# Strassen's algorithm for all columns of w_down, with accumulating transfers for two of the weight sums

## The chip, the core and the metric

The kernel runs on one core of a Trainium2 chip. The metric is the device time of one execution in microseconds (us). The engines named below are PE (the matrix engine, fed by PEld's weight loads), DVE (elementwise on two inputs), ACT (elementwise on one input, casts), POOL (a general engine) and SP (a queue that issues transfers).

## The reference

An encoder of two layers over 256 tokens of width 2048. The mixers of a layer (projection, three kinds of attention, output projection) are the same before and after the change. What it touches is the MLP that follows them:

```python
h = rmsnorm(x, norm_mlp[l])
u = jax.nn.relu(jnp.einsum('bsd,df->bsf', h, w_up[l]))     # 2048 -> 8192
x = x + jnp.einsum('bsf,fd->bsd', u * u, w_down[l])        # 8192 -> 2048
```

All of it is in float32.

## The kernel before

**Precision.** Every operand of a matmul is split into two parts of a shorter float format (fp32r): hi, a cast on ACT, and lo, the rest, a subtraction on DVE. A product is then three matmuls: hi times hi, lo times hi, hi times lo.

**Steps.** The kernel is one list of steps. A step takes one 512 KB piece of weights (128 partitions x 1024 columns), and does the matmuls with it. The main loop over the steps (from L1016) issues, at step i, the loads of step i + 6 (`load`, SP's queue), the split of the weights of step i + 2 (`split`, L988 the cast into `whi`, L989 the subtraction into `wlo`; each has three buffers), the `prep` of step i + 4 where there is one, and then the matmuls of step i. The framework places the instructions of each engine in a fixed order from this, by their dependences and its own times, so that neighbours can change places; each engine then runs its list in order.

**Groups.** The 8192 hidden columns are worked in eight groups of 1024 per layer. A group's u comes from 16 up steps (four blocks q of 256 columns, four steps each; 8 matmuls of 512 columns, L691, and 8 of 256 columns, L696). After each fourth up step the block is taken out of its two PSUM banks: L668 to L676 form u squared and its two parts, and `sums_of` (L707) forms four sums of u's blocks for Strassen's algorithm. These make up the left operand of w_down in the next round. While group g of w_down is worked, the up steps of group g + 1 run between.

**w_down.** For columns 1024 to 2047 (j = 2, 3) a group has 8 plain steps of 12 matmuls (`mode_b`, L477), which add in two banks per j, then L739 adds them to x. For columns 0 to 1023 of groups 0 to 6 the product of u (2 blocks of 128 tokens by 2 parts of the group's rows) and of the weights (2 parts by 2 column blocks of 512) is done by Strassen's algorithm in Winograd's form, with 7 products instead of 8 (`strassen_steps`). Each product has two steps of 6 matmuls (h = 0, 1, the halves of its rows; L802), and adds up in bank a or d, which share the tile S, or in a bank of its own (P2). After its second step L782 adds it to x, or subtracts it. Products in the order P1, P6, P7, P5, P3, P2, P4; a later product on the same bank goes on adding to what the bank holds. The right operands are weights or sums of them: B12 + B11, B22 + B11 + B12, B12 + B22 and B21 added to the second, all made by DVE (L815, L817, L821, L832) for h = 0 and h = 1.

The raw weights lie in `wraw` (five buffers, up and plain steps), `side` (four buffers: B12, B22, B21) and `spare` (one for each h: B11). `mm_bank` gives one of six banks. `t2` and the parts of u lie in `big` (24 buffers).

**Order of a group before.** 0 is an up or plain step, 1 a step of a product; one round per product:

```python
order = [0, 0]
for p_ in range(7):
    order += [1, 0, 1] + ([0, 0] + [0] * (p_ in (1, 3, 5)) if p_ < 6 else [])
```

Group 7 has plain steps alone, in both versions.

Of the kernel before, what the change touches and what calls it, by code (L numbers as in the profile page):

```python
# [23 lines left out]
P = 128  # L24
# [19 lines left out]
def tile_trunk(ctx: ExitStack, tc: tile.TileContext, x_in, w_in, w_o, w_up, w_down,  # L44
# [459 lines left out]
    def layer_steps(l):  # L504
# [152 lines left out]
        def up_steps(g):  # L657

            out_, evacs = [], []
            for q in range(4 * g, 4 * g + 4):  # L660
                box = {}

                def evac(q=q, box=box):
                    need(("rrow", l))
                    a = mid(F32, 2, 256)
                    for i in range(2):

                        nc.scalar.copy(a[:, i, :], box["b"][i][:, 256:512])  # L668
                        nc.vector.tensor_add(a[:, i, :], a[:, i, :], box["b"][i][:, 0:256])
# [6 lines left out]
                    nc.vector.tensor_sub(u[:, 1], a, f(u[:, 0]))  # L676
                    uT[q] = u
                    if q < 28:
                        sums_of(q, a)
# [27 lines left out]
        def sums_of(q, a):  # L707

            v = a.rearrange("p k (t c) -> p (k t) c", t=2)
            sm = mid(F32, 4, P)  # L710
            a11, a21, a12 = v[:, 0, :], v[:, 1, :], v[:, 2, :]
            nc.vector.tensor_sub(sm[:, 0:2, :], v[:, 0:4:3, :], v[:, 1:2, :].to_broadcast([P, 2, P]))
            nc.vector.scalar_tensor_tensor(sm[:, 2, :], sm[:, 1, :], -1.0, a11, op0=ALU.mult, op1=ALU.subtract)
            nc.vector.scalar_tensor_tensor(sm[:, 3, :], sm[:, 2, :], -1.0, a12, op0=ALU.mult, op1=ALU.subtract)
# [5 lines left out]
        def down_steps(g, js):  # L720
            out_ = []
            for j in js:
                box = {}
                for k in range(4):
                    def mm(wh, wl, j=j, k=k, box=box):
                        if k == 0:
                            box["b"] = [mm_bank(), mm_bank()]
                            box["w"] = []
                        final = l == L - 1 and g == 7 and j == 3
                        hts = [uT[4 * g + k]] * 2  # L730
                        mode_b(box["b"], hts, wh, wl, [0, 1], k == 0, k == 3, blocks=(0,) if final else (0, 1),
                               lo_last=g < 7)
# [7 lines left out]
                        if final:  # L740
                            evac(0)
                            final_block(0)
                            tail = [mm_bank(), mm_bank()]
                            for c in range(2):
                                cols = slice(c * 256, c * 256 + 256)
                                for i, (hts, vh, vl) in enumerate(box["w"]):
                                    mode_b([None, tail[c]], hts, vh[:, :, cols], vl[:, :, cols], [0, 1],
                                           i == 0, i == 3, n=256, blocks=(1,))
# [9 lines left out]
                    out_.append(Step(w_down[l, (g * 4 + j) * 4 + k], 2, 512, None, mm, fourth=g == 7))  # L758
            return out_

        def strassen_steps(g):

            raw, t2, box = {}, {}, {}

            def src(par, j, h):
                return w_down[l, g * 16 + (par * 2 + j) * 2 + h]  # L770

            def left(name, q):

                if name[0] == "A":
                    t, kk = int(name[1]) - 1, int(name[2]) - 1
                    return [uT[q][:, i, kk, t * P:(t + 1) * P] for i in range(2)]
                return [sT[q][:, i, "3124".index(name[1]), :] for i in range(2)]

            def evac(bank, t, j, sign):
                xs = x[:, t, j * 512:(j + 1) * 512]  # L780
                op = nc.vector.tensor_add if sign > 0 else nc.vector.tensor_sub
                op(xs, xs, bank)  # L782


            plan = [("P1", "A11", "a", True, (0, 0, 1)), ("P6", "S2", "a", False, (1, 0, 1)),
                    ("P7", "S3", "d", True, (1, 1, -1)), ("P5", "S1", "a", False, (1, 1, -1)),
                    ("P3", "S4", "a", False, (0, 1, -1)), ("P2", "A12", "b", True, (0, 0, 1)),
                    ("P4", "A22", "d", False, (1, 0, 1))]
            out_ = []
            for name, lf, bk, fresh, dst in plan:  # L790
                for h in range(2):
                    def mm(wh, wl, name=name, lf=lf, bk=bk, fresh=fresh, dst=dst, h=h):
                        if (name, h) == ("P1", 0):
                            pair = score_banks().rearrange("p (b i) n -> p b (i n)", i=2)
                            box["a"], box["d"] = pair[:, 0], pair[:, 1]
                        if (name, h) == ("P2", 0):
                            box["b"] = mm_bank()
                        o = box[bk]
                        ops = [left(lf, 2 * h + i + 4 * g) for i in range(2)]
                        for a, w in ((0, wh), (1, wh), (0, wl)):  # L800
                            for i in range(2):
                                nc.tensor.matmul(o, ops[i][a], w[:, i, :], skip_group_check=True,  # L802
                                                 start=fresh and h == 0 and i == 0 and a == 0 and w is wh,
                                                 stop=h == 1 and i == 1 and w is wl)
                        if h == 1:
                            evac(o, *dst)
                    loads, prep, get = [], None, None
                    if name == "P1":
                        loads = [(("B11", h), src(0, 0, h), lambda h=h: spare(F32, h))]
                        get = lambda h=h: raw["B11", h]  # L810
                    elif name == "P6":
                        loads = [(("B12", h), src(0, 1, h), None), (("B22", h), src(1, 1, h), None)]

                        def prep(h=h):
                            nc.vector.tensor_add(raw["B11", h], raw["B11", h], raw["B12", h])  # L815
                            t2[h] = big(F32, 2, 512)
                            nc.vector.tensor_add(t2[h], raw["B22", h], raw["B11", h])  # L817
                        get = lambda h=h: t2[h]
                    elif name == "P7":
                        def prep(h=h):  # L820
                            nc.vector.tensor_add(raw["B12", h], raw["B12", h], raw["B22", h])  # L821
                        get = lambda h=h: raw["B12", h]
                    elif name == "P5":
                        get = lambda h=h: raw["B11", h]
                    elif name == "P3":
                        get = lambda h=h: raw["B22", h]
                    elif name == "P2":
                        loads = [(("B21", h), src(1, 0, h), None)]
                        get = lambda h=h: raw["B21", h]
                    else:  # L830
                        def prep(h=h):
                            nc.vector.tensor_add(t2[h], raw["B21", h], t2[h])  # L832
                        get = lambda h=h: t2[h]
                    stp = Step(None, 2, 512, None, mm, fourth=False, prep=prep, raw=get,
                               loads=[(raw, k, v, w) for k, v, w in loads])
                    out_.append(stp)
            return out_

        steps.extend(up_steps(0))
        for g in range(7):  # L840
            ss = down_steps(g, (2, 3)) + up_steps(g + 1)
            hs = strassen_steps(g)

            order = [0, 0]
            for p_ in range(7):
                order += [1, 0, 1] + ([0, 0] + [0] * (p_ in (1, 3, 5)) if p_ < 6 else [])
            assert order.count(0) == len(ss) and order.count(1) == len(hs), (order.count(0), order.count(1))
            steps.extend(hs.pop(0) if o else ss.pop(0) for o in order)
        steps.extend(down_steps(7, range(4)))

    def layer_end(l, j):
        if l + 1 < L:
# [254 lines left out]

def _pack_down(w, g):

    plain = [_pack(w[:, j * 512:(j + 1) * 512], 2) for j in range(4)]  # L1110
    if g < 7:
        b = w.reshape(8, P, D)
        plain[0:2] = [np.stack([b[[4 * h + par, 4 * h + par + 2], :, j * 512:(j + 1) * 512].transpose(1, 0, 2).reshape(P, 1024)
                                for j in range(2) for h in range(2)]) for par in range(2)]
    return np.concatenate(plain)


def _pack_inputs(inp):
# [56 lines left out]
```

## Time and profile before

| | |
|---|---|
| time, median of 3 runs | 2019.84 us (2019.82 to 2021.61) |
| the profiled execution | 2019.96 us, its span 2018.2 us |
| PE busy | 2003.0 us, 99% of the span |
| DVE busy | 1644.0 us, 81% |
| ACT busy | 1208.2 us, 60% |
| POOL busy | 257.2 us, 13% |
| transfers | 381.28 MB, mean 189 GB/s, the main queue 59.0% of 16 engines |

Instructions of one engine are listed with start and length; a matmul's or a DVE instruction's end lies over the start of the next one, so that what it costs in a full row is the distance between two starts. A row of a stretch gives the busy time of each engine in that part of the span. In groups by line the last part of a row is the idle time of the engine just before these instructions, and what ended it.

### The profile page before, as it was taken

What the parts mean: (1) busy time and instruction counts of PE and PEld (TensorE: products, weight loads), DVE (VectorE), ACT (ScalarE), POOL (GpSimd) and SP (SyncE); (2) the same over time, 40 slices, a digit from 0 to 9 for tenths busy, and PEclk for the clock granted to TensorE, in tenths of its full rate; (3) what the DMA queues carried; (4) which work ended last, traced back from release to release, by engine and by line L of the source; (5) the groups of instructions that cost most, each with busy time, mean ns of one, the idle gap of its engine ahead of it and who ended that gap; (6) DMA issues with size and microseconds to landing.
All of it is one profiled execution on the core that took longest, in us unless ns stands there. A gap on an engine that the chain in (4) does not pass through costs nothing.

```text
span 2018.2 us, 27873 instructions
## 1 busy us (share of the span) xinstructions
PE 2003.0 (99%) x10264; PEld 1707.6 (85%) x10264; DVE 1644.0 (81%) x2095; ACT 1208.2 (60%) x1748; POOL 257.2 (13%) x296
## 2 busy tenths in 40 slices
PE   9999999999999999999999999999999999999998
PEld 7888788888888888888888888888888888888887
DVE  6777977879888898887658789778888888888975
ACT  6667756565555556555656676565655556565554
POOL 0493330000000000000005744200000000000001
PEclk9999999999999999999999999999999999999999
DMA  8655465566565756656656455565665756657554
GB/s 279 197 167 154 165 190 188 175 212 191 184 222 171 223 186 190 213 173 199 188 179 185 156 165 175 180 188 181 194 210 174 231 167 209 203 170 235 165 166 156
DMA packets 108821, 381.28 MB, mean 189 GB/s; under 512 B 12259, under 2 KB 16611, under 8 KB 108684
## 3 DMA queue, kind: packets, MB, share of 16 engines
q1 hardware_dynamic: 108252, 378.41, 59.0%
q8 instruction: 80, 1.31, 0.2%
q10 hardware_dynamic: 432, 1.10, 0.1%
q14 instruction: 57, 0.47, 0.1%
HBM read 377.34 MB, written 2.11 MB: 188 GB/s over the span
## 4 chain that ended last, share of the span: by engine, by line
PE 93%; DVE 3%; ACT 1%; POOL 1%; issue 1%; DMA 1%; SPq 0%; DVEq 0%; POOLq 0%
PE mm L477 40%; PE mm L691 23%; PE mm L696 12%; PE S L802 11%; PE mm L802 2%; PE tr L392 1%; PE tr L219 1%; POOL big L939 1%; DVE wlo L989 1%; PE tr L411 1%; ACT big L372 1%; DVE big L287 1%; PE S L351 1%; PE S L350 1%; DVE big L394 0%
## 5 line engine op out<-in xcount | busy, mean ns | idle before, releaser
L988 ACT CAST whi<-wraw 128x1024 fp32r<-128x1024 f32 (+1 forms) x531 | 556.9, 1051 | 421.9 <-PE mm L691 170.2
L989 DVE TENSOR_TENSOR wlo<-wraw,whi 128x1024 fp32r<-128x1024 f32 (+1 forms) x531 | 655.9, 1237 | 184.7 <-ACT whi L988 181.8
L477 PE MATMUL mm<-whi,big 128*128 128x512 f32 (+1 forms) x2252 | 643.8, 386 | 0.3 <-ACT whi L988 0.3
L691 PE MATMUL mm<-big,whi 128*128 128x512 f32 x2048 | 509.6, 391 | 0.0
L477 PEld LDWEIGHTS mm<-whi,big 128*128 128x128 f32 x2252 | 419.0, 188 | 82.9 <-ACT whi L988 2.3
L691 PEld LDWEIGHTS mm<-big,whi 128*128 128x128 f32 x2048 | 377.4, 188 | 73.7
L477 PE MATMUL mm<-wlo,big 128*128 128x512 f32 (+1 forms) x1126 | 375.7, 385 | 1.0 <-DVE wlo L989 1.0
L696 PEld LDWEIGHTS mm<-big,wlo 128*128 128x128 f32 x2048 | 279.5, 191 | 19.9
L696 PE MATMUL mm<-big,wlo 128*128 128x256 f32 x2048 | 285.7, 283 | 0.0
L477 PEld LDWEIGHTS mm<-wlo,big 128*128 128x128 f32 x1126 | 212.0, 188 | 41.8 <-DVE wlo L989 2.3
L802 PE MATMUL S<-whi,big 128*128 128x512 f32 x672 | 182.3, 393 | 0.0
L477 PE MATMUL mm<-spare,big 128*128 128x512 f32 (+1 forms) x678 | 158.5, 382 | 0.0
L988 ACT CAST whi<-side 128x1024 fp32r<-128x1024 f32 x84 | 88.3, 1051 | 95.5 <-PE mm L691 78.0
L477 PEld LDWEIGHTS mm<-spare,big 128*128 128x128 f32 x678 | 122.3, 188 | 23.1
L802 PEld LDWEIGHTS S<-whi,big 128*128 128x128 f32 x672 | 119.2, 189 | 18.6
L989 DVE TENSOR_TENSOR wlo<-side,whi 128x1024 fp32r<-128x1024 f32 x84 | 102.6, 1222 | 37.2 <-ACT whi L988 36.9
L383 POOL TENSOR_SCALAR big<-big,sm 128x256 f32<-128x256 f32 x128 | 89.4, 716 | 247.0 <-DVE sm L381 208.9
L255 POOL TENSOR_TENSOR sm<-sm,mhalf 128x2 f32<-128x2 f32 (+2 forms) x14 | 13.4, 954 | 793.5 <-DVE sm L250 773.6
L988 ACT CAST whi<-big 128x1024 fp32r<-128x1024 f32 x56 | 58.9, 1052 | 85.3 <-DVE big L817 36.4
L802 PE MATMUL S<-wlo,big 128*128 128x512 f32 x336 | 104.0, 391 | 0.0
L870 POOL TENSOR_TENSOR x<-x,big 128x512 f32<-128x512 f32 x6 | 8.6, 1456 | 669.5 <-ACT mid L877 669.5
L988 ACT CAST whi<-spare 128x1024 fp32r<-128x1024 f32 x56 | 59.0, 1053 | 47.8 <-PE mm L691 27.8
(152 smaller groups left out, 2093.8 us busy)
## 6 DMA issues: line engine op xcount, KB each, us to landing
wraw<-in_w_up_dram SPq DMA_DIRECT2D x256, 512.0 KB, 4.2
wraw<-in_w_down_dram SPq DMA_DIRECT2D x144, 512.0 KB, 3.7
wraw<-in_w_in_dram SPq DMA_DIRECT2D x119, 512.0 KB, 3.8
side<-in_w_down_dram SPq DMA_DIRECT2D x84, 512.0 KB, 4.3
wraw<-in_w_o_dram SPq DMA_DIRECT2D x64, 512.0 KB, 3.9
spare<-in_w_down_dram SPq DMA_DIRECT2D x28, 512.0 KB, 4.3
side<-in_rpb_dram SPq DMA_DIRECT2D x32, 174.8 KB, 5.0
side<-avec SPq DMA_DIRECT2D x8, 384.0 KB, 5.2
```

The lines of the kernel that those rows point to most:

```text
L219: tr = nc.tensor.transpose(psv[:, kk, t, :], x[:, t, c0:c0 + P], ident).ins
L287: nc.vector.tensor_sub(kl[rows, par::2, :], z, f(kh[rows, par::2, :]))
L350: nc.tensor.matmul(o, st, u.kh[:, kh, :], start=True, stop=False)
L351: nc.tensor.matmul(o, st, u.kl[:, kh, :], start=False, stop=True)
L372: nc.scalar.activation(p[:, s, :], src[s], AF.Exp, bias=negm[:, s:s + 1], scale=u.rq[:, s:s + 1] if u.kind == "C" else 1.0, accum_out=sums ...
L383: nc.gpsimd.tensor_scalar(p[:, s, :], p[:, s, :], rs[:, s:s + 1], 1.0, op0=ALU.mult, op1=ALU.mult)
L477: return nc.tensor.matmul(banks[t][:, 0:n], a, (wl if part == "hl" else wh)[:, i, :], start=first and i == 0 and part == "hh", stop=last a ...
L691: nc.tensor.matmul(box["b"][fs], wh[:, kk, fs * P:(fs + 1) * P], ht, start=s == 0 and kk == 0, stop=False, skip_group_check=True)
L696: nc.tensor.matmul(box["b"][fs][:, 0:256], wl[:, kk, fs * P:(fs + 1) * P], ht[:, 0:256], start=False, stop=s == 3 and kk == 3, skip_group_ ...
L802: nc.tensor.matmul(o, ops[i][a], w[:, i, :], skip_group_check=True, start=fresh and h == 0 and i == 0 and a == 0 and w is wh, stop=h == 1 ...
L988: act = nc.scalar.copy(h[:, part], w[:, part]).ins
L989: last_lo[0] = nc.vector.tensor_sub(lo[:, part], w[:, part], f(h[:, part])).ins
```

## The change

All 2048 columns of w_down in groups 0 to 6 now go by Strassen's algorithm, as two halves of 1024 columns one after the other. A group has 28 product steps and 16 up steps, where it had 14 product steps, 8 plain steps and 16 up steps.

- The products run in the order P1, P2, P7, P6, P5, P3, P4. Per half the order is product, up, product for each of them; one more up step stands between the halves, and the last product of the second half has none between its two steps.
- Two of the four sums of weights are made by transfers that POOL issues and that add the weights in memory onto the tile: B12 is loaded a second time onto B11 (at P2's prep, once P1's split has read B11), and B21 a second time onto t2 (at P5's prep, once P6's split has read t2). DVE makes the other two (P7's and P6's prep).
- P2 of each half keeps one PSUM bank (`own`) through groups 0 to 6 and is added to x once, in group 6.
- The blocks of u are stored in another order, so that the three blocks that are needed unsummed lie side by side: the cast and the subtraction for u cover 384 of 512 columns in groups 0 to 6.

The diff, cut to its core:

```diff
-                    u = big(F32R, 2, 2, 256)
-                    nc.scalar.copy(u[:, 0], a)
-                    nc.vector.tensor_sub(u[:, 1], a, f(u[:, 0]))
+                    u = big(F32R, 2, 512)
+                    n, af = 384 if q < 28 else 512, a.rearrange("p k c -> p (k c)")
+                    nc.scalar.copy(u[:, 0, 0:n], af[:, 0:n])
+                    nc.vector.tensor_sub(u[:, 1, 0:n], af[:, 0:n], f(u[:, 0, 0:n]))
...
-        def strassen_steps(g):
+        own = {}
+        def strassen_steps(g, half):
...
-            plan = [("P1", "A11", "a", True, (0, 0, 1)), ("P6", "S2", "a", False, (1, 0, 1)),
-                    ("P7", "S3", "d", True, (1, 1, -1)), ("P5", "S1", "a", False, (1, 1, -1)),
-                    ("P3", "S4", "a", False, (0, 1, -1)), ("P2", "A12", "b", True, (0, 0, 1)),
+            plan = [("P1", "A11", "a", True, (0, 0, 1)), ("P2", "A12", "b", True, (0, 0, 1)),
+                    ("P7", "S3", "d", True, (1, 1, -1)), ("P6", "S2", "a", False, (1, 0, 1)),
+                    ("P5", "S1", "a", False, (1, 1, -1)), ("P3", "S4", "a", False, (0, 1, -1)),
                     ("P4", "A22", "d", False, (1, 0, 1))]
+            def on_top(tile, par, j, h):
+                nc.gpsimd.dma_start(tile, src(par, j, h).rearrange("p (k n) -> p k n", k=2), accum_op=ALU.add)
...
-                        if (name, h) == ("P2", 0):
-                            box["b"] = mm_bank()
-                        o = box[bk]
+                        if (name, h, g) == ("P2", 0, 0):
+                            own[half] = mm_bank()
+                        o = own[half] if bk == "b" else box[bk]
...
-                        if h == 1:
+                        if h == 1 and (bk != "b" or g == 6):
                             evac(o, *dst)
...
+                    elif name == "P2":
+                        loads = [(("B21", h), src(1, 0, h), None)]
+                        def prep(h=h):
+                            on_top(raw["B11", h], 0, 1, h)
+                    elif name == "P7":
+                        loads = [(("B12", h), src(0, 1, h), None), (("B22", h), src(1, 1, h), None)]
+                        def prep(h=h):
+                            nc.vector.tensor_add(raw["B12", h], raw["B12", h], raw["B22", h])
                     elif name == "P6":
-                        loads = [(("B12", h), src(0, 1, h), None), (("B22", h), src(1, 1, h), None)]
                         def prep(h=h):
-                            nc.vector.tensor_add(raw["B11", h], raw["B11", h], raw["B12", h])
                             t2[h] = big(F32, 2, 512)
                             nc.vector.tensor_add(t2[h], raw["B22", h], raw["B11", h])
-                    elif name == "P7":
-                        def prep(h=h):
-                            nc.vector.tensor_add(raw["B12", h], raw["B12", h], raw["B22", h])
+                    elif name == "P5":
+                        def prep(h=h):
+                            on_top(t2[h], 1, 0, h)
...
-                        def prep(h=h):
-                            nc.vector.tensor_add(t2[h], raw["B21", h], t2[h])
...
-            ss = down_steps(g, (2, 3)) + up_steps(g + 1)
-            hs = strassen_steps(g)
+            ss = up_steps(g + 1)
+            hs = strassen_steps(g, 0) + strassen_steps(g, 1)
             order = [0, 0]
-            for p_ in range(7):
-                order += [1, 0, 1] + ([0, 0] + [0] * (p_ in (1, 3, 5)) if p_ < 6 else [])
+            for p_ in range(14):
+                order += [1, 0, 1] + [0] * (p_ == 6) if p_ < 13 else [1, 1]
```

The weights are packed in memory to match.

More of the change, by code (lines that the diff above doesn't have):

```diff
@@ L718, in sums_of, with down_steps @@
             sT[q] = t
-        def down_steps(g, js):
+        def down_steps(g):
             out_ = []
-            for j in js:
+            for j in range(4):
                 box = {}
@@ L757, in mm @@
                             layer_end(l, j)
-                    out_.append(Step(w_down[l, (g * 4 + j) * 4 + k], 2, 512, None, mm, fourth=g == 7))
+                    out_.append(Step(w_down[l, (g * 4 + j) * 4 + k], 2, 512, None, mm))
             return out_
-        def strassen_steps(g):
-            raw, t2, box = {}, {}, {}
+        own = {}
+        def strassen_steps(g, half):
+            raw, t2, box, done = {}, {}, {}, set()
             def src(par, j, h):
-                return w_down[l, g * 16 + (par * 2 + j) * 2 + h]
+                return w_down[l, g * 16 + half * 8 + (par * 2 + j) * 2 + h]
             def left(name, q):
                 if name[0] == "A":
-                    t, kk = int(name[1]) - 1, int(name[2]) - 1
-                    return [uT[q][:, i, kk, t * P:(t + 1) * P] for i in range(2)]
-                return [sT[q][:, i, "3124".index(name[1]), :] for i in range(2)]
+                    b = ("12", "22", "11").index(name[1:]) * P
+                    return [uT[q][:, i, b:b + P] for i in range(2)]
+                return [sT[q][:, i, "1324".index(name[1]), :] for i in range(2)]
             def evac(bank, t, j, sign):
-                xs = x[:, t, j * 512:(j + 1) * 512]
+                xs = x[:, t, half * 1024 + j * 512:half * 1024 + (j + 1) * 512]
                 op = nc.vector.tensor_add if sign > 0 else nc.vector.tensor_sub
                 op(xs, xs, bank)
-            plan = [("P1", "A11", "a", True, (0, 0, 1)), ("P6", "S2", "a", False, (1, 0, 1)),
-                    ("P7", "S3", "d", True, (1, 1, -1)), ("P5", "S1", "a", False, (1, 1, -1)),
-                    ("P3", "S4", "a", False, (0, 1, -1)), ("P2", "A12", "b", True, (0, 0, 1)),
+            plan = [("P1", "A11", "a", True, (0, 0, 1)), ("P2", "A12", "b", True, (0, 0, 1)),
+                    ("P7", "S3", "d", True, (1, 1, -1)), ("P6", "S2", "a", False, (1, 0, 1)),
+                    ("P5", "S1", "a", False, (1, 1, -1)), ("P3", "S4", "a", False, (0, 1, -1)),
                     ("P4", "A22", "d", False, (1, 0, 1))]
+            def on_top(tile, par, j, h):
+                nc.gpsimd.dma_start(tile, src(par, j, h).rearrange("p (k n) -> p k n", k=2), accum_op=ALU.add)
             out_ = []
@@ L802, in mm @@
                                 nc.tensor.matmul(o, ops[i][a], w[:, i, :], skip_group_check=True,
-                                                 start=fresh and h == 0 and i == 0 and a == 0 and w is wh,
+                                                 start=fresh and h == 0 and i == 0 and a == 0 and w is wh
+                                                 and (bk != "b" or g == 0),
                                                  stop=h == 1 and i == 1 and w is wl)
-                        if h == 1:
+                        if h == 1 and (bk != "b" or g == 6):
                             evac(o, *dst)
@@ L826, in strassen_steps, with operand @@
                         get = lambda h=h: raw["B22", h]
-                    elif name == "P2":
-                        loads = [(("B21", h), src(1, 0, h), None)]
-                        get = lambda h=h: raw["B21", h]
-                    else:
-                        def prep(h=h):
-                            nc.vector.tensor_add(t2[h], raw["B21", h], t2[h])
+                    else:
                         get = lambda h=h: t2[h]
-                    stp = Step(None, 2, 512, None, mm, fourth=False, prep=prep, raw=get,
+                    def operand(get=get, key=(name, h)):
+                        done.add(key)
+                        return get()
+                    stp = Step(None, 2, 512, None, mm, fourth=False, prep=prep, raw=operand,
                                loads=[(raw, k, v, w) for k, v, w in loads])
@@ L1108, in _pack_down @@
 def _pack_down(w, g):
[L1110 to L1115, printed above, removed]
+    if g == 7:
+        return np.concatenate([_pack(w[:, j * 512:(j + 1) * 512], 2) for j in range(4)])
+    b = w.reshape(8, P, D)
+    return np.stack([b[[4 * h + par, 4 * h + par + 2], :, (2 * half + j) * 512:(2 * half + j + 1) * 512]
+                     .transpose(1, 0, 2).reshape(P, 1024)
+                     for half in range(2) for par in range(2) for j in range(2) for h in range(2)])
 def _pack_inputs(inp):
```

27 lines of the change are left out of this document (14 added, 13 removed).

## The prediction

> **What bounds the kernel now.** I read the shares of the engines first, then the stretches of the MLP, then groups by line, then the timelines around one group.
>
> ```profile
> PE 2003.0 (99%) x10264; PEld 1707.6 (85%) x10264; DVE 1644.0 (81%) x2095; ACT 1208.2 (60%) x1748; POOL 257.2 (13%) x296
> PE 93%; DVE 3%; ACT 1%; POOL 1%; issue 1%; DMA 1%; SPq 0%; DVEq 0%; POOLq 0%
> 645.50:731.00 85.50, 85.50 (x437) 73.17 (x436) 73.67 (x90) 49.15 (x59) 0.00 (x0) 1.00 0.62 197
> sum 342.00, PE 342.00 PEld 292.70 DVE 294.68 ACT 196.59 POOL 0.00; mean PE 85.50 PEld 73.17 DVE 73.67 ACT 49.15 POOL 0.00
> ```
>
> The third row is one MLP group of layer 0, the fourth four groups in a row (columns: length, then PE, PEld, DVE, ACT, POOL busy, granted clock, DMA share, GB/s). A group lasts 85.50 us, PE has no gap in it at full clock, and DVE works 73.67, so 11.8 us of each group are its margin. POOL does nothing there. 14 of 16 groups are changed (0 to 6 in two layers): 1197 of the 2018.2 us.
>
> **The change part by part.**
>
> *Matmuls.* A plain step of w_down issues 12 matmuls, a product's step 6. Per group the change takes away 8 plain steps (96 matmuls) and adds 14 product steps (84). Timeline of PE, start and length:
>
> ```profile
> 645.51 1.98 PE L477 MATMUL mm<-whi,big 128*128 128x512 f32 x8
> ...
> 648.23 1.98 PE L477 MATMUL mm<-whi,big 128*128 128x512 f32 x8
> ...
> 662.03 2.00 PE L691 MATMUL mm<-big,whi 128*128 128x512 f32 x8
> ...
> 664.82 1.09 PE L802 MATMUL S<-whi,big 128*128 128x512 f32 x4
> ...
> 666.21 1.98 PE L691 MATMUL mm<-big,whi 128*128 128x512 f32 x8
> ```
>
> From start to start a plain step takes 2.72, an up step 2.79, a product step 1.39 (1.36 where a plain step precedes: I take 1.375). 8 x 2.72 = 21.76 goes, 14 x 1.375 = 19.25 comes: 2.5 us less per group, so PE needs 83.0. Fourteen times that is 35 us, the most the change can bring.
>
> *Splits.* Each step of w_down is cast on ACT (L988) and subtracted on DVE (L989): six steps more per group. DVE in a dense stretch:
>
> ```profile
> 670.44 0.42 DVE L712 TENSOR_TENSOR mid<-mid 128x256 f32<-128x256 f32 x1
> 670.78 0.69 DVE L676 TENSOR_TENSOR big<-mid,big 128x512 fp32r<-128x512 f32 x1
> 671.38 0.28 DVE L713 SCALAR_TENSOR_TENSOR mid<-mid,mid 128x128 f32<-128x128 f32 x1
> 671.59 0.68 DVE L782 TENSOR_TENSOR x<-x,S 128x512 f32<-128x512 f32 x1
> 672.18 0.28 DVE L714 SCALAR_TENSOR_TENSOR mid<-mid,mid 128x128 f32<-128x128 f32 x1
> 672.38 1.22 DVE L989 TENSOR_TENSOR wlo<-wraw,whi 128x1024 fp32r<-128x1024 f32 x1
> 673.52 1.22 DVE L989 TENSOR_TENSOR wlo<-side,whi 128x1024 fp32r<-128x1024 f32 x1
> ```
>
> Lengths overlap the next start by 0.08: 1024 columns cost 1.14, 512 cost 0.60, 256 cost 0.34, 128 cost 0.20. DVE: 6 x 1.14 = +6.8. ACT: 6 x 1.05 = +6.3 on 49.15, hidden in 83.
>
> *Sums of weights, additions to x, operands of u.* Over four groups:
>
> ```profile
> L782 DVE TENSOR_TENSOR x<-x,S 128x512 f32<-128x512 f32 x24 | 16.3, 680 | 0.0
> L782 DVE TENSOR_TENSOR x<-x,mm 128x512 f32<-128x512 f32 x4 | 2.7, 680 | 0.0
> L739 DVE TENSOR_TENSOR x<-x,mm 128x512 f32<-128x512 f32 x16 | 10.5, 680 | 0.0
> L832 DVE TENSOR_TENSOR big<-side,big 128x1024 f32<-128x1024 f32 x8 | 9.8, 1226 | 8.8 <-DMA side<-in_w_down_dram 8.8
> L815 DVE TENSOR_TENSOR spare<-spare,side 128x1024 f32<-128x1024 f32 x8 | 9.7, 1218 | 0.0
> ```
>
> DVE forms four sums for each of two row halves now (L832, L815 and two lines like them), 8 per group. Afterwards it forms two, for each row half of two column halves: 8 again. Additions to x go from 11 (24 + 4 + 16 over four) to 12, as P2 adds only once, in group 6: +0.6. The subtraction for u covers 384 of 512 columns, 4 x 0.60 x 1/4 = -0.6; ACT's cast shrinks alike. DVE: 73.67 + 6.8 + 0.6 - 0.6 = 80.5 in 83.0. Its margin falls from 11.8 to 2.5 us. That is the price of the change.
>
> *The dense place of a half.* The order repeats product, up, product. From the end of P1's second step to the end of P7's second step PE has four product steps and two up steps, 4 x 1.375 + 2 x 2.79 = 11.1. In that time DVE must do six splits (6.8), four sums (4.6), the addition for P1 (0.6) and one u with its sums: counting up steps, one ends in this place in each half. A u costs 2 x 0.34 + 0.60 + 0.45 + 0.34 + 2 x 0.20 + 0.60 = 3.1. Together 15.1, 4.0 over. How far DVE can be ahead, from PE, ACT and DVE:
>
> ```profile
> 703.71 1.09 PE L802 MATMUL S<-whi,big 128*128 128x512 f32 x4
> 704.64 0.62 PE L802 MATMUL S<-wlo,big 128*128 128x512 f32 x2
> 704.84 1.05 ACT L988 CAST whi<-wraw 128x1024 fp32r<-128x1024 f32 x1 [0.83 <-PE S L802]
> 705.92 1.23 DVE L989 TENSOR_TENSOR wlo<-wraw,whi 128x1024 fp32r<-128x1024 f32 x1 [0.66 <-ACT whi L988]
> ```
>
> A buffer freed as the wlo part starts (704.64) holds the weights of the third step after it 2.5 us later, 2.05 after its step ends (705.09). That later step starts 2.79 + 1.375 = 4.17 after this end and wants wlo 0.9 later still: a lead of 3.0 us. Of the 4.0 over, 3.0 are covered, and a sum or two can go ahead of time. I take 0.6 us of PE stall per half (ends: 0, all sums early, and 1.6, one split late besides), 1.2 per group. The next four products use less DVE than PE time and restore the lead.
>
> *Loads on SP.* Still 32 per group, but B12 and B22 of the second row half now reuse the two buffers that P2's B21 leaves, of four. The same turn of a buffer can be read before:
>
> ```profile
> 648.66 1.23 DVE L989 TENSOR_TENSOR wlo<-side,whi 128x1024 fp32r<-128x1024 f32 x1
> 649.91 0.33 SPq L968 DMA_DIRECT2D side<-in_w_down_dram  x1
> 654.65 1.23 DVE L832 TENSOR_TENSOR big<-side,big 128x1024 f32<-128x1024 f32 x1 [1.30 <-DMA side<-in_w_down_dram]
> ```
>
> From the freeing split to the use are 4.8 us after SP issues. Behind P2's second split (at the earliest 2.05 after P1's second step) this lands 6.8 after that step; the sum then takes 1.2 and the cast 1.1, so P7's second step could start at 9.1 and its turn is at 9.7 (11.1 - 1.4). Hidden, by 0.6. SP holds later loads behind these waits: the next up load lands one transfer later (1.7, the price worked out below), 8.5 after P1's second step, and its step is due at 12.5. DVE's own wait, 8.8 over four groups, is 2.2 per group now; I leave it as it is, and with 80.5 it fills 82.7 of 83.0.
>
> *Accumulating transfers on POOL.* Eight per group: B12 added onto B11 once P1's split has read it, used nine steps later by P6's sum; B21 added onto t2 once P6's split has read it, used nine steps later by P4. Nine steps, six products and three ups, are 16.6 us. POOL holds only these, in the order of their use, so a waiting one delays the next and nothing else.
>
> ```profile
> wraw<-in_w_up_dram SPq DMA_DIRECT2D x256, 512.0 KB, 4.2
> x<-in_x_dram SPq DMA_DIRECT2D x8, 256.0 KB, 7.0
> ```
>
> The trace holds no such transfer. The nearest row below is a plain load, 4.2 us; above, the slowest rate in the trace, 7.0 for half the bytes, so 14. Both fit in 16.6, and I take 0. For bandwidth: 0.62 of 85.50 is 53.0 us for 32 loads, 1.66 each. At that price 40 transfers use 66 of 83.0. PE stays the bound up to (83.0 - 53.0) / 8 = 3.75 each, 2.3 loads' worth. The Trainium skill, DMA: Bandwidth & Descriptors, Rules for kernel authors, says that an accumulate reads its destination and writes it later; counted as two loads, my estimate by that rule is 79.6 of 83.0, still under, but with little left; no row of before bears on it.
>
> Does POOL slow DVE? The subtraction while POOL is busy (from 100 us on), and in a group:
>
> ```profile
> 100.00:200.00 100.00, 99.53 (x508) 84.18 (x507) 77.38 (x102) 70.40 (x131) 66.29 (x71) 1.00 0.53 162
> L989 DVE TENSOR_TENSOR wlo<-wraw,whi x12: 1207/1286/1636, 103.9 to 148.4; 128x1024 fp32r<-128x1024 f32 x12
> L989 DVE TENSOR_TENSOR wlo<-wraw,whi x25: 1215/1224/1227, 644.5 to 730.0; 128x1024 fp32r<-128x1024 f32 x25
> ```
>
> Medians 1286 against 1224 ns with POOL two thirds busy: if each of the eight issues touched two of the 52 wide DVE instructions of a group, 16 x 0.06 = 1.0 us; ends 0 and 1.0. I take 0, as POOL is idle otherwise (0.00 busy in the group). The Trainium skill, SBUF — State Buffer, Who interferes with whom, has a DVE instruction with two SBUF inputs contend with GpSimd reads; the trace agrees, by these 62 ns. By that rule the sum stays at 0, since it infers that writing descriptors needs only the write side.
>
> *Bank kept by P2.* Two of six banks are held through seven groups; four remain for the ups, which use two per q and had three steps to free them. 0; if this cover failed, PE would wait one u (3.1) per q.
>
> **The sum.** 83.0 + 1.2 = 84.2 per group, 1.3 less, times 14 is 18 us. Span 2018.2 - 18 = 2000, and the profiled run lay 1.8 above its span (2019.96, with a median of 2019.84 over three): 2002.
>
> **The rivals.**
>
> *Bank a passed on at once (slower).* In before, every second step of a product is followed by an up or plain step, so its addition to x is covered. Now P6's second step is followed directly by P5's first, and P5's by P3's, on the same bank: four times per group PE must wait for DVE's 0.60, plus on average half of a 1.14 already running: 4 x 1.17 = 4.7, 87.7 per group, +31 us, 2051. It decides above 0.62 per place. Against it: the next up step's matmuls can be put ahead, 8 of 0.23, if its whi is there. That instructions are put out of the code's order is seen on DVE:
>
> ```profile
> 714.23 0.42 DVE L712 TENSOR_TENSOR mid<-mid 128x256 f32<-128x256 f32 x1
> 714.57 1.22 DVE L815 TENSOR_TENSOR spare<-spare,side 128x1024 f32<-128x1024 f32 x1
> 715.70 0.28 DVE L713 SCALAR_TENSOR_TENSOR mid<-mid,mid 128x128 f32<-128x128 f32 x1
> ```
>
> L815 belongs to a later step, yet stands inside the u of an earlier one. On PE no row shows it, as nothing called for it. Chance 0.16.
>
> *DVE becomes the bound (slower).* It needs 80.5; above 5.0 us of idle per group it is slower than before. The 2.2 of DMA waits, 1.6 in each half from a late split, and 1.0 from POOL give 80.5 + 2.2 + 3.2 + 1.0 = 86.9: +20 us, 2040. Chance 0.12.
>
> *The transfers become the bound.* Above 3.75 us of DMA time each, say 5: 93, +105 us, 2125. Chance 0.03.
>
> *Nothing is won.* 2.5 us of stalls eat the matmuls, 85.5: 2020. Chance 0.08.
>
> *Everything fits.* 83.0: 1985; the low end of the forecast.
>
> **How the numbers follow.** Forecast 0.61, its own range 1985 to 2014 (stall 0 to 2.1). With the second rival, and part of the first, 1985 to 2045 leaves out some 0.15. Three runs spread 0.09%, so 0.2% (4 us) is about what can be told from no change. Faster 0.61, same 0.08, slower 0.31.
>
> **What would show it.** Groups of 84.2 in the stretches; PE busy near 99% of them, with its waits before P7's second step; DVE over 80 of a group; PE groups on a product's line running between halves of an up step; accumulates landing within 14 us. The forecast is wrong if PE waits for the addition to x at P5 and P3, if DVE idles over 5 us per group, or if the DMA share passes 0.95.

## The result and the profile after

| | median | ratio to before, 95% interval | one changed group |
|---|---|---|---|
| before | 2020.07 us | | 85.50 us |
| changed kernel | 2205.64 us | 1.0917 [1.0902, 1.0931] | 98.97 us |

The change costs 9.2%: the forecast of 2002 us was wrong in sign, and the time lies far above the range. The page's first row of engines and the row of the chain, of the changed kernel:

```profile
PE 2053.1 (93%) x10096; PEld 1707.1 (77%) x10096; DVE 1743.2 (79%) x2197; ACT 1281.3 (58%) x1832; POOL 356.6 (16%) x408
PE 72%; DMA 11%; DVE 9%; ACT 4%; issue 2%; POOL 0%; DVEq 0%; SPq 0%; POOLq 0%; ACTq 0%
```

PE was 99% busy and 93% of the chain; now it is 93% busy, and a quarter of the chain lies with transfers, DVE and ACT. PE's busy time has grown by 50 us although it has 168 matmuls fewer. The stretches of the changed kernel say both in one place (length, then PE, PEld, DVE, ACT, POOL busy, granted clock, DMA share, GB/s). The first row is a whole group; the others are the place after P7's second step in the next half:

```profile
584.35:683.32 98.97, 89.47 (x425) 73.40 (x425) 80.55 (x97) 54.44 (x65) 6.99 (x8) 0.95 0.72 213
683.90:687.80 3.90, 0.15 (x1) 0.00 (x0) 3.87 (x7) 2.60 (x4) 0.00 (x0) 0.86 0.42 134
687.80:694.00 6.20, 6.14 (x18) 5.13 (x19) 3.67 (x4) 2.00 (x3) 1.75 (x2) 0.54 0.60 100
694.00:730.00 36.00, 36.00 (x182) 30.24 (x181) 28.59 (x33) 20.22 (x24) 1.74 (x2) 1.00 0.85 252
```

Of the group's 98.97 us PE stands still for 98.97 - 89.47 = 9.5 and works 89.47 where 83.0 would do, 6.5 more. Some 5 of these are the lowered clock, an estimate from the group's mean of 0.95 (0.05 x 98.97). The clock falls after each of the two long stops, but not equally: after the group's first stop, as after the one shown in the third row, it is 0.54 over 6.2 us; after the second, from 638.45 on, 0.72 over as long. DVE's work is 80.55 us, as forecast, and yet it is idle for 18.4. For the other 36 us of this half PE has no gap at all (in the half before it, one of 0.68 us): the loss lies in one place of each half. Here is that place, engine by engine (start, length, and in brackets the idle time before and what ended it). The first row holds the splits of P2's second and P7's first operand; the second row's first load is B22 for P7's second step:

```profile
672.64 2.60 DVE L1006 TENSOR_TENSOR wlo<-side,whi 128x1024 fp32r<-128x1024 f32 x2
673.90 1.69 SPq L985 DMA_DIRECT2D side<-in_w_down_dram  x2
679.51 1.23 DVE L831 TENSOR_TENSOR side<-side,side 128x1024 f32<-128x1024 f32 x1 [2.02 <-DMA side<-in_w_down_dram]
680.85 1.05 ACT L1005 CAST whi<-side 128x1024 fp32r<-128x1024 f32 x1 [4.07 <-DVE side L831]
681.95 1.20 PE L810 MATMUL S<-whi,big 128*128 128x512 f32 x4 [0.34 <-ACT whi L1005]
680.66 0.74 DVE L669 TENSOR_TENSOR mid<-mid,mm 128x256 f32<-128x256 f32 x2
682.16 0.73 ACT L673 ACTIVATE mid<-mid,zero 128x512 f32<-128x512 f32 x1 [0.26 <-DVE mid L670]
684.30 0.29 DVE L716 SCALAR_TENSOR_TENSOR mid<-mid,mid 128x128 f32<-128x128 f32 x1
684.51 1.22 DVE L836 TENSOR_TENSOR big<-side,spare 128x1024 f32<-128x1024 f32 x1
685.82 1.04 ACT L1005 CAST whi<-big 128x1024 fp32r<-128x1024 f32 x1 [0.57 <-DVE big L836]
686.77 1.04 ACT L1005 CAST whi<-wraw 128x1024 fp32r<-128x1024 f32 x1
687.86 3.78 PE L693 MATMUL mm<-big,whi 128*128 128x512 f32 x8 [3.81 <-ACT whi L1005]
691.44 1.48 PE L698 MATMUL mm<-big,wlo 128*128 128x256 f32 x6
```

Read from the top: the split of P2 frees a buffer, SP issues B22 at once (673.90), it lands 5.5 us later, and DVE has waited 2.0 us for it. P7's second step itself is late by only 0.34 us. But the sum L831 holds up what stands behind it on DVE: the work for a block of u (L669, L670, then over ACT's L673 back to L714 to L716), and behind that P6's sum (L836). On ACT the cast of P6's operand waits for that sum, and the cast of the next up step (686.77), whose weights lay ready, stands behind it. PE, whose list has the up step first, waits 3.81 us for that cast, and then takes 3.6 us for eight matmuls that take 1.82 elsewhere.

### The profile page after: what moved, and what is told of

It is laid out like the page before. It is cut to its first block, busy times and chain, and to the rows that moved or that the text cites. A ratio compares the mean times of both kernels' runs of the same rounds, so it can differ in the third digit from the quotient of the medians.

```text
span 2203.8 us, 28224 instructions
## 1 busy us (share of the span) xinstructions
PE 2053.1 (93%) x10096; PEld 1707.1 (77%) x10096; DVE 1743.2 (79%) x2197; ACT 1281.3 (58%) x1832; POOL 356.6 (16%) x408
## 4 chain that ended last, share of the span: by engine, by line
PE 72%; DMA 11%; DVE 9%; ACT 4%; issue 2%; POOL 0%; DVEq 0%; SPq 0%; POOLq 0%; ACTq 0%
PE mm L477 23%; PE mm L693 19%; PE S L810 17%; DMA side<-in_w_down_dram 11%; PE mm L698 9%; DVE wlo L1006 4%; ACT whi L1005 3%; DVE side L831 1%; PE tr L392 1%; DVE mid L669 1%; PE tr L219 1%; PE tr L411 1%; ACT big L372 1%; PE S L351 0%; PE S L350 0%
## 5 line engine op out<-in xcount | busy, mean ns | idle before, releaser
L693 PE MATMUL mm<-big,whi 128*128 128x512 f32 x2048 | 561.9, 414 | 107.7 <-ACT whi L1005 107.7
L1006 DVE TENSOR_TENSOR wlo<-wraw,whi 128x1024 fp32r<-128x1024 f32 (+1 forms) x419 | 520.0, 1243 | 153.7 <-ACT whi L1005 150.7
L1005 ACT CAST whi<-wraw 128x1024 fp32r<-128x1024 f32 (+1 forms) x419 | 438.1, 1048 | 286.6 <-PE mm L693 104.1
L477 PE MATMUL mm<-whi,big 128*128 128x512 f32 (+1 forms) x1356 | 422.3, 384 | 1.4 <-ACT whi L1005 1.4
L810 PE MATMUL S<-whi,big 128*128 128x512 f32 x1344 | 376.6, 402 | 18.3 <-ACT whi L1005 17.9
L810 PEld LDWEIGHTS S<-whi,big 128*128 128x128 f32 x1344 | 237.9, 193 | 75.4 <-ACT whi L1005 23.0
L477 PEld LDWEIGHTS mm<-whi,big 128*128 128x128 f32 x1356 | 250.6, 188 | 50.1 <-ACT whi L1005 4.0
L477 PE MATMUL mm<-wlo,big 128*128 128x512 f32 (+1 forms) x678 | 255.7, 381 | 1.0 <-DVE wlo L1006 1.0
L1006 DVE TENSOR_TENSOR wlo<-spare,whi 128x1024 fp32r<-128x1024 f32 x112 | 136.8, 1221 | 75.7 <-PE S L810 72.1
L1006 DVE TENSOR_TENSOR wlo<-big,whi 128x1024 fp32r<-128x1024 f32 x112 | 135.7, 1221 | 32.1 <-ACT whi L1005 32.0
L810 PEld LDWEIGHTS S<-wlo,big 128*128 128x128 f32 x672 | 124.4, 188 | 43.9 <-DVE wlo L1006 17.6
```

The costliest lines, as they stand in the source:

```text
L477: return nc.tensor.matmul(banks[t][:, 0:n], a, (wl if part == "hl" else wh)[:, i, :], start=first and i == 0 and part == "hh", stop=last a ...
L693: nc.tensor.matmul(box["b"][fs], wh[:, kk, fs * P:(fs + 1) * P], ht, start=s == 0 and kk == 0, stop=False, skip_group_check=True)
L1005: act = nc.scalar.copy(h[:, part], w[:, part]).ins
L1006: last_lo[0] = nc.vector.tensor_sub(lo[:, part], w[:, part], f(h[:, part])).ins
```

## Experiments

The theories. A: the late load for P7's second step starts this chain, because the side buffers must first be left by P2's B21. B: DVE, with 80.5 us of work in 83, is simply too full. C: the accumulating transfers are the cause. Beside them stands the question what the slow clock costs. After the first three runs two more came: D, that it is the order in which work stands on DVE and ACT, with u in the wrong place, and E, that the dense place is short of DVE time in whatever order.

| run | what | median us | ratio, 95% interval | one group, us |
|---|---|---|---|---|
| e1_b21_wraw | B21 in the ring of wraw | 2104.29 | 1.041 [1.0395, 1.0426] | 91.4 |
| e2_dummies | PE's wait filled | 2191.21 | 1.0845 [1.0827, 1.0863] | 96.4 |
| e3_no_accum | accumulating transfers left out | 2158.14 | 1.0682 [1.0666, 1.0698] | 94.9 |
| e4_b21_noacc | e1 and e3 together | 2098.40 | 1.0384 [1.0364, 1.0403] | |
| e5_one_first | e1, u made later | 2012.03 | 0.9962 [0.9947, 0.9977] | 84.8 |
| e6_three_first | e1, u made earlier | 2081.91 | 1.0304 [1.0289, 1.0319] | 91.9 |
| e7_order_alone | the order of e5 alone | 2075.06 | 1.0274 [1.0259, 1.029] | 88.4 |
| e8_no_p7_sums | e5 without P7's sums | 2000.30 | 0.9902 [0.9887, 0.9917] | 84.0 |
| e9_up_before_p6 | e1, up step ahead of P6 | 2053.18 | 1.016 [1.0143, 1.0177] | 87.5 |

The last column is a single group of the profiled run; the mean over the 14 groups can differ. By the spans it is 85.50 + (2079.4 - 2018.2) / 14 = 89.9 for e6, and 89.7 for e7.

### The late load alone

```diff
-                        loads = [(("B21", h), src(1, 0, h), None)]
+                        loads = [(("B21", h), src(1, 0, h),
+                                  lambda: wp.tile([P, 2, 512], F32, tag="wraw", bufs=5, name=nm("wraw")))]
```

> Edit: P2's B21 is loaded into the ring of wraw (five buffers, otherwise only up steps in these groups) instead of the ring of side (four). The four side buffers then hold B12 and B22 alone, and the loads for P7's second step no longer wait for a split of P2. Theory A (the late load starts a chain: sum L831 waits for its transfer, P6's sum and the cast of the next up step stand behind it on DVE and ACT, PE waits 3.8 us, and then runs at about half clock): the wait and the slow stretch go, in the trace of the changed kernel 0.2 to 1.2 + 0.17 + 3.81 + about 2.7 us per half, 28 halves, 190 to 220 us, so 1990 to 2025 us. Theory B (DVE is simply too full, 80.5 us of work per group): PE waits somewhere else instead, 2100 us or more. Theory C (the accumulating transfers hold the loads up): the landing stays late and the time stays within 2% of 2205.

More than half of the loss is gone (101 of 186 us), and DVE no longer waits for that load. But 2104 is not the 1990 to 2025 of theory A, and B's bound of 2100 fits the number. The same place in this run, two rows of DVE, three of ACT, one of PE, and two stretches behind such waits:

```profile
658.48 0.68 DVE L670 SCALAR_TENSOR_TENSOR mid<-mid,rrow 128x512 f32<-128x512 f32 x1
659.20 0.72 ACT L673 ACTIVATE mid<-mid,zero 128x512 f32<-128x512 f32 x1 [1.89 <-DVE mid L670]
661.29 1.22 DVE L837 TENSOR_TENSOR big<-side,spare 128x1024 f32<-128x1024 f32 x1
662.60 1.04 ACT L1006 CAST whi<-big 128x1024 fp32r<-128x1024 f32 x1 [0.57 <-DVE big L837]
663.55 1.04 ACT L1006 CAST whi<-wraw 128x1024 fp32r<-128x1024 f32 x1
664.64 3.37 PE L693 MATMUL mm<-big,whi 128*128 128x512 f32 x8 [2.46 <-ACT whi L1006]
664.60:668.00 3.40, 3.36 (x9) 2.66 (x10) 3.40 (x4) 0.94 (x1) 0.87 (x1) 0.58 0.16 14
710.50:714.00 3.50, 3.43 (x17) 2.81 (x18) 3.50 (x4) 2.03 (x3) 0.88 (x1) 1.00 0.31 19
```

The second half of the chain is still there without a late load: u's work goes from DVE to ACT and back, ACT idles 1.89 us for it, and P6's sum, its cast and the up step's cast follow. PE waits 2.46 us in each half.

### The slow clock

```diff
+                        if (name, h) == ("P7", 1):
+                            for _ in range(16):
+                                nc.tensor.matmul(own[half], warm[:, 0:P], warm, start=False, stop=False, skip_group_check=True)
```

> Edit: behind the matmuls of P7's second step, 16 more matmuls that add zeros onto P2's bank, so that PE works (about 3.65 us) where it waits 3.81 us for the next up step's cast. 448 matmuls more, nothing else changed. Theory of the clock (the granted clock falls to 0.54 for the 6 us after the wait because PE stood still): the wait stays in length but is filled, the matmuls after it run at 0.23 us per 512 columns again, and the time falls by 28 x 2.5, about 70 us, to about 2135. Rival (the matmuls behind the wait are slow because of what they wait for, buffers or transfers, or the clock falls for the power of what went before): no gain, 2205, or a loss of up to 28 x 3.65 = 100 us, 2305, if the filling adds to the wait.

```profile
588.75 2.11 PE L693 MATMUL mm<-big,whi 128*128 128x512 f32 x8 [0.16 <-ACT whi L1008]
588.75:685.19 96.44, 93.32 (x456) 76.18 (x456) 80.97 (x97) 55.00 (x65) 7.00 (x8) 1.00 0.72 218
```

The wait is filled (0.16 is left of 3.81), the clock stays at 1.00 in this group and the eight matmuls take 1.95 us to the next start again. That PE's standing still lowers the clock is shown. But the time falls by 14 us, not 70. PE's matmuls other than the fillers take 2053.1 - (2115.9 - 112.3) = 49.5 us less in all. The fillers, 112.3 us, take 16 more than the waits that they fill (107.7 us before, 11.5 left), and PE's waits ahead of the products' matmuls (for casts, lo parts and additions to x) grow from 24.1 to 43.1 us. What PE regains is mostly lost again at the next operand. The clock is a symptom, and little of its price reaches the time while the waits stay.

### The accumulating transfers

```diff
-                nc.gpsimd.dma_start(tile, src(par, j, h).rearrange("p (k n) -> p k n", k=2), accum_op=ALU.add)
+                pass
```

> Edit: the accumulating transfers are left out (the sums that they make are left out of the result); everything else stands. 58.7 MB less are moved and POOL issues nothing in the MLP. Theory A (the late load alone): the side loads still wait for P2's splits; the landing gets shorter by what the queues share, some 0.3 us of 4.5, and the time falls by at most 28 x 0.5 = 14 us, 2190 to 2206. Theory C (the accumulating transfers are the cause, by their bandwidth, by holding up the loads or through POOL beside DVE): back to 1990 to 2030.

> Edit: P2's B21 in the ring of wraw, as in the first run, and the accumulating transfers left out (their sums are left out of the result). Leaving them out of the changed kernel brought 47 us. If that came from the late side load alone (they made it land later), nothing is left to win here: 2095 to 2105, against 2104. If they cost something of their own (bandwidth, POOL beside DVE, P5's and P4's operands landing late), the 47 us come again: about 2057.

Left out of the changed kernel, they bring 47 us, more than A's 14 and far from C's 175 or more. Left out where the late load has gone already, they bring 2104.3 - 2098.4 = 6, and the two intervals overlap. So nearly all of their cost runs through that load, and I had its size wrong: without them DVE waits 23.8 / 28 = 0.9 us for it each time, with them 61.5 / 27 = 2.3. The rows of the queues in the changed kernel, and DVE's waits for the load there and without the accumulating transfers (us in total, times, longest):

```profile
q1 hardware_dynamic: 108252, 378.41, 50.3%
q0 software_dynamic: 16128, 58.73, 15.6%
...
side<-in_w_down_dram SPq DMA_DIRECT2D x168, 512.0 KB, 4.5
...
spare<-in_w_down_dram POOLq DMA_DIRECT2D x56, 512.0 KB, 6.4
big<-in_w_down_dram POOLq DMA_DIRECT2D x56, 512.0 KB, 6.7
```

```profile
DVE side L831 <- DMA side<-in_w_down_dram: 61.5, 27, 3.6
```

```profile
DVE side L831 <- DMA side<-in_w_down_dram: 23.8, 28, 1.6
```

An accumulating transfer takes 0.156 x 2203.8 / 112 = 3.07 us of the 16 engines; a load (722 pieces of 512 KB in the first row) takes 0.503 x 2203.8 / 722 = 1.54. That is twice as much.

### Order, with the late load gone

```diff
-            order = [0, 0]
+            order = [0]
             for p_ in range(14):
-                order += [1, 0, 1] + [0] * (p_ == 6) if p_ < 13 else [1, 1]
+                order += [1, 0, 1] + [0] * (p_ == 6)
```

> Edit: P2's B21 in the ring of wraw, and one up step instead of two at the start of a group; the last product gets one between its two steps instead. Every fourth up step, behind which a block of u is made, moves from beside P2 (step 4 of a half) to beside P7 (step 7) and from beside P3 (16) to beside P4 (19). Theory D (the work for u passes between DVE and ACT four times, stands on both ahead of P6's sum and of the cast of the next up step, and PE waits 2.47 us for that, per half): with u made later, behind those, the wait goes or moves: 2030 to 2075. Rival E (the dense place is short of DVE time, in whatever order): u's work still falls before P6 ends, and the wait stays within 0.5 us: 2090 to 2115.

The time is 2012, below D's range and 0.38% below the kernel before. Nothing was taken away: the same steps, with u's work now beside P7 and P4 instead of P2 and P3. A whole group, PE's one wait of note in a half, and the place where bank a is handed on from P5 to P3:

```profile
606.32:691.14 84.82, 84.19 (x424) 70.35 (x425) 79.87 (x97) 54.66 (x64) 6.98 (x8) 1.00 0.87 247
648.71 1.21 PE L698 MATMUL mm<-big,wlo 128*128 128x256 f32 x8 [0.31 <-DVE wlo L1007]
...
652.76 1.52 PE L693 MATMUL mm<-big,whi 128*128 128x512 f32 x6
654.12 1.20 PE L810 MATMUL S<-whi,big 128*128 128x512 f32 x4
655.15 0.62 PE L810 MATMUL S<-wlo,big 128*128 128x512 f32 x2
655.61 0.63 PE L693 MATMUL mm<-big,whi 128*128 128x512 f32 x2
```

DVE works 79.87 of 84.82 us, 94%, and keeps up. B falls, and E with it. Six matmuls of the next up step stand ahead of the product that waits for its bank, the other two behind it: the cover that the prediction hoped for.

The opposite shift, u made earlier:

```diff
-            order = [0]
+            order = [0, 0, 0]
             for p_ in range(14):
-                order += [1, 0, 1] + [0] * (p_ == 6)
+                order += [1] + [0] * (p_ < 12) + [1] + [0] * (p_ == 6)
```

> Edit: P2's B21 in the ring of wraw, and three up steps at the start of a group; P3 and P4 of each half have none between their two steps in the second half's end only (12 of the 14 products keep theirs). A block of u then ends beside P1 (step 1) and beside P5 (step 13). Theory D, and E as well: u's work is done before the sums for P7 and P6 come, so the wait of 2.47 us and the slow clock behind it go, 28 x (2.5 + 1 to 2), about 100 us: 2000 to 2040, less what five product steps in a row at the end of a group cost (0 to 2 us per group). If the residue is neither (hand-over of bank a, DVE's fullness over the whole group): 2080 or more.

```profile
626.22 1.16 PE L810 MATMUL S<-whi,big 128*128 128x512 f32 x4 [2.62 <-ACT mid L673]
630.44 2.11 PE L693 MATMUL mm<-big,whi 128*128 128x512 f32 x8 [1.25 <-ACT whi L1006]
634.73 1.72 PE L810 MATMUL S<-whi,big 128*128 128x512 f32 x4 [2.18 <-DVE x L786]
```

The 2.46 us of each half are gone, but new waits have come once per group: three in the group shown, 6 us together, and over the 14 groups 40.2 us ahead of a product's step (2.62 in most groups), 10.5 for additions to x and 9.7 for casts of up steps, 4.3 per group. 2082 is outside the 2000 to 2040 of D and E, and lies where I had put a residue that is neither. This order differs in two ways at once, u's place and five product steps in a row, so it does not tell which of them made the new waits.

### The second link, and the order alone

```diff
-                order += [1, 0, 1] + [0] * (p_ == 6) if p_ < 13 else [1, 1]
+                order += ([0, 1, 1] if p_ in (3, 10) else [1, 0, 1]) + [0] * (p_ == 6) if p_ < 13 else [1, 1]
```

> Edit: the kernel with B21 in the ring of wraw and the old order (2104), with the up step that stood between P6's two steps put ahead of both (up, product, product for P6 alone). Its cast then stands on ACT ahead of P6's, which waits for DVE's sum. Theory D in its second link (PE's 2.47 us are the up step's cast standing behind P6's): the wait for that cast goes, and P6's operand comes while the up step runs (2.8 us): 2025 to 2060. If the whole chain is late for other reasons: 2090 or more.

```profile
607.50 1.22 DVE L837 TENSOR_TENSOR big<-side,spare 128x1024 f32<-128x1024 f32 x1
609.24 1.22 DVE L837 TENSOR_TENSOR big<-side,spare 128x1024 f32<-128x1024 f32 x1
611.51 0.68 DVE L786 TENSOR_TENSOR x<-x,S 128x512 f32<-128x512 f32 x1
612.34 1.15 PE L810 MATMUL S<-whi,big 128*128 128x512 f32 x4 [1.44 <-DVE x L786]
```

With the up step's cast ahead of P6's, 51 of the 84 us by which the kernel with B21 in wraw was slower than before are gone, as expected. What is left is a wait of 1.44 us ahead of P6's own step: by the trace it ends with P7's addition to x, which stands on DVE behind P6's two sums. P6's operand was cast before that. P6 and P7 have different banks, but both belong to the tile S; why the one waits for the other's addition was not taken apart.

> Edit: the changed kernel with the order of the run that came out at 2012 (one up step at the start of a group, the last product with one between its steps), and B21 back in the ring of side. If the late side load costs the 101 us that its removal brought in the old order whatever the order is, 2100 to 2115. If the two act together (the late sum does its harm through the work for u that stands between it and the next up step's cast, and that work has moved away), less than half of it is left: 2015 to 2060.

```profile
609.58:697.96 88.38, 85.90 (x424) 70.29 (x424) 80.28 (x97) 53.98 (x65) 6.99 (x8) 1.00 0.83 238
609.58 1.20 PE L810 MATMUL S<-whi,big 128*128 128x512 f32 x4 [1.26 <-ACT whi L1005]
612.02 2.10 PE L693 MATMUL mm<-big,whi 128*128 128x512 f32 x8 [0.45 <-ACT whi L1005]
```

2075 lies between the two forecasts, and neither held. The late load still costs 2075.1 - 2012.0 = 63 us in this order, against 101 in the old one: some 60% of its harm does not need u in its old place. The new order gains 131 us with the late load and 92 without it. In this group, whose waits are at most 1.26 us, the clock stays at 1.00.

### What is left

```diff
                     elif name == "P7":
...
-                        def prep(h=h):
-                            nc.vector.tensor_add(raw["B12", h], raw["B12", h], raw["B22", h])
                         get = lambda h=h: raw["B12", h]
```

> Edit: the kernel that came out at 2012 (B21 in the ring of wraw, one up step first) without P7's sums, which are left out of the result: 4 additions of 1.14 less on DVE per group, 79.9 down to 75.3 of 84.8. PE alone needs 83.0. If the last 1.8 us per group are DVE's fullness (a wait of 0.31 for wlo, twice per group, and the additions to x that P5 and P3 wait for coming late), most goes: 1986 to 2000. If they are the hand-over of bank a by itself, they stay: 2005 to 2012.

```profile
614.04:698.00 83.96, 83.96 (x425) 70.77 (x426) 76.35 (x93) 54.55 (x64) 6.99 (x8) 1.00 0.86 251
```

In this stretch of 83.96 us, about a group long, PE has no gap, and DVE is busy for 76.35. By the spans a group takes 85.50 - (2018.2 - 1997.7) / 14 = 84.0 us, 1.0 above the 83.0 forecast for PE. The median, 2000.30, lies at the upper edge of the first case, 1986 to 2000. The run takes away, with the sums, the wait of P7's casts for them, so the 12 us between the two medians are an upper bound for what DVE's fullness costs in e5. The remaining 1.0 us was not taken apart.

## Why the prediction was wrong

- **Matmuls: right within about 1 us.** 83.0 us per group; the two best runs come to 84.0 and 84.8 for a group, with PE busy nearly throughout.
- **DVE's work: right.** 80.5 forecast, 80.55 measured. That it fits was right too, but only in another order.
- **Loads on SP: the first step that failed.** The load was issued 2.08 us after P1's second step (2.05 forecast), landed after 5.5 us where I took 4.8 from before, and P7's step started 0.34 late where I had a margin of 0.6. So far a miss of 1 us. The error was to stop there. I wrote "DVE's own wait ... I leave it as it is". It did not stay at 2.2 us per group but came to 61.5 / 14 = 4.4, and, which weighs more, in an engine that runs its list in order, the 2.0 us before the sum delay u's work, P6's sum, two casts and an up step. I had asked what waits for the sum, not what stands behind it.
- **The dense place: mis-sized.** 0.6 us per half forecast, with ends of 0 and 1.6. With the late load away PE still lost 2.46 us there, because u's work passes between DVE and ACT, and each waits for the other while holding up what is behind it. I had added up DVE's time, which was right, and not the passing. With u elsewhere, 0.31 is left.
- **The clock: missing.** Nothing in the prediction priced a wait of PE beyond its length. In the group shown it adds some 5 us of slow matmuls to 9.5 us of waits, though filling the waits won back only 14 us in all. The Trainium skill, TensorE: Matmul & The Clock Gate, HAM oscillation, names gaps over about 3.4 us as what lowers the clock; 3.81 us and 0.54 agree, but in e1 waits of 2.46 us did it too, after 12 of 23 (0.58 in the place shown).
- **Accumulating transfers: the direct part right, the indirect wrong.** They land in 6.4 and 6.7 us, far within 16.6, and in the changed kernel no wait ends with one of them. The upper bound of 14 was misread, without effect: 7.0 us for 256 KB is not the slowest rate in the trace of before, where 160 KB took 7.3, and at that rate 512 KB would take 23 us and not fit. But 47 us hang on what they add to another load's landing. Each costs two loads' DMA time; the Trainium skill, DMA: Bandwidth & Descriptors, Rules for kernel authors, has the accumulate read its destination before it writes it; twice the time fits that, but no row shows the read itself.
- **The rivals.** The hand-over of bank a is covered by an up step, as argued against that rival. That DVE becomes the bound is refuted by e5. One sign of being wrong did come, DVE idle for over 5 us per group (18.4), but from waits and not from too much work. The case that came was none of my list, though its pieces were: I gave each a price of its own and no price to their standing in one line.

The forecast for a group, 84.2, is close to what the same work takes in e5 (84.8). The change was priced rightly as work and wrongly as a schedule.

## What to carry to other kernels

When an engine's margin shrinks (here DVE's, from 11.8 to about 5 us of a group even in the best order), price a late operand by everything that stands behind its consumer in that engine's list, across engines, and not by its consumer alone. Two loops to look for: a buffer that is refilled only after another consumer has left it, and a chain that passes between two in-order engines near the densest place. Moving either can be worth more than the work that was saved: 101 and 92 us here, against the 35 that the seven products bring at most.

## What the runs showed of the hardware

- In the changed kernel all 22 stops of PE of 3.81 us were followed by a lowered granted clock, over the next 6.2 us 0.53 to 0.59 after 7 of them and 0.72 to 0.74 after 15.
- Shorter stops lowered it in some places and not in others: 2.46 us in e1 after 12 of 23. After 25 stops of 1.44 us in e9 it stayed at 1.00, but after one of 1.39 in e2, at 727.75, it was 0.72 over 6.2 us. In these runs the length of a stop alone does not decide it.
- An accumulating transfer takes 3.07 us of DMA time for 512 KB, a plain load 1.54, and POOL 0.87 us to issue.
